# A mixer layer on one core: the last o block copied out between shifted blocks, the tail of g_b as one list, v and z in single transfers

## The chip, the cores and the metric

The kernel runs on one core of a Trainium2 chip, in one launch. The metric is the device time of one execution in microseconds. A core has five engines, each of which executes its own list of instructions in order and waits at semaphores for the others: TensorE (PE in the profile), VectorE (DVE), ScalarE (ACT), GpSimd (POOL) and SyncE (SP), whose list here consists of DMA issues.

## The reference, cut to what matters

512 prompt rows and 32 sample rows of width 2048 go through one layer. All weights are float32.

```python
h = rmsnorm(x, norm_w) * (1 + scl) + shift
q, k, v, o, z_a, ifg, u, z_b, g_a, g_b = split_cols(h @ w_in)
hm, c1, n1, m1 = mlstm_sequence(heads(q), heads(k) * DH ** -0.5, heads(v), ig, lf, c0, n0, m0)   # 4 heads of 512
a  = silu(z_a) * head_layernorm(sigmoid(o) * hm, head_norm_w)
pb, new_hist = pool_mixer(u, hist, pos0, w_pool_mix, pool_scale)   # 4 groups of 256 columns, windows 2, 4, 8, 16
bb = silu(z_b) * pb
merged = sigmoid(g_a) * (a @ w_branch_a) + sigmoid(g_b) * (bb @ w_branch_b)
y = rmsnorm(x + gate * (merged @ w_out), final_norm_w)
```

In `pool_mixer` a group takes the mean over its window of the last inputs (15 rows of history stand ahead of the first), subtracts the input and multiplies by a 256 x 256 matrix.

## The kernel before

Everything is kept with features on partitions and the T = 544 rows (512 + 32) along the free axis, in two halves of 272. A float32 product is made of three matmuls: `split` (L90 to L92) casts a tile to a high part on ACT and subtracts it on DVE for the low part, and PE adds up high x high, low x high and high x low in PSUM. This is done for weights (`whi`, `wlo`) and for activations (`h_hi`, `h_lo`) alike. A column block is 128 outputs wide; one with 16 k-tiles takes 16 x 3 x 2 = 96 matmuls. PSUM has a pool "mm" of two slots with two banks each, for the sums of a block, and a pool "ax" of four single banks, which `aux` hands out.

The stages follow one another in program order:

- Head 0 of k, q, v and o through `project` (L108 to L131), on h without its shift; their shift is added later as a bias. Each block's sums are copied to `ot` by ACT (L411) and stored to `d_p` from POOL's queue (L412).
- The shift of h: 16 k-tiles `hx` on DVE, split in place into `h_hi` and `h_lo` (L468 to L473), with PE taking up each tile at once for the input and forget gates (L477) and for the first two blocks of g_a (L484); the second half of block 1 follows at L491. Their weights come from `parts` (`whi` and `wlo`, 128 x 1024), with rows loaded by `load_rows`.
- Three more pairs of g_a blocks by `plain_pair` (L518), then the rest of the projection by `fast_pair` (L639, L651), which needs fewer products.
- The tail: the last four blocks of g_b, 12 to 15, again by `plain_pair` (L840 to L848). After a block its `evac` makes the sigmoid and calls `pool_group` (L782 to L839) for groups 0 and 1 behind block 13, for group 2 behind block 14 and for group 3 behind block 15. `pool_group` transposes the history and the last inputs on PE (`tp`, L797, L804, L805), sums the window on DVE (`lv`, one addition per doubling), subtracts (`dd`), splits (`d_hi`, `d_lo`), multiplies on PE into `mixed` (L834) and writes `zb` times `mixed` (L837) and its split `b_hi`, `b_lo`.
- The heads stage: blocks of branch_b (L1048), the filler, stand between the parts of each of the four heads: scores, `values` (transposes of v to rows, L948 and L952, out of tiles `vt`), `mix` (L961, L962), output gates from `o4`, norm, and `finish_head`, which multiplies by `zg`.
- The tiles `af` of the first three heads are read back and split (L1151), then branch_a and w_out.

The Tile framework puts the instructions of each engine in a list and the waits between them. A tile of a pool waits until the last user of its buffer is done. A DMA issue of SP that has to wait for its buffer holds every issue behind it in that list.

## Time and profile before

| what | value |
|---|---|
| median of 3 runs | 2283.69 us (2277.29, 2287.27, 2283.69) |
| the profiled execution | 2276.01 us |
| its span | 2274.2 us |
| mean granted clock of TensorE | 0.989 |
| busy share PE, DVE, ACT, POOL | 97 %, 72 %, 39 %, 5 % |
| mean DMA rate | 163 GB/s |

The span runs from the first to the last instruction of the profiled execution; its own time is 1.8 us more. A busy share is an average over all stages. The clock column of a window is TensorE's granted clock as a share of 2.4 GHz, the upper of its two levels; half of it is 1.2 GHz.

### The profile page before, as it was taken

The numbers are of one execution on the slowest core, as the hardware profiler recorded it, in microseconds if no ns is written. First come the engines' busy times: TensorE is split into PE (matmuls) and PEld (weight loads), VectorE is DVE, ScalarE is ACT, GpSimd is POOL, SyncE is SP. The second block draws the span as 40 slices with busy tenths as digits, with TensorE's granted clock in tenths as the row PEclk, the third lists the DMA queues.
The fourth block names the chain that finished last, engine by engine and source line by source line (L and its number), as shares of the span: only waits on it lengthen the run. The fifth ranks groups of instructions, "written<-read, shape, count | busy, mean of one in ns | idle before, by whom it ended". The sixth has DMA issues, their size and how long they took to land.

```text
span 2274.2 us, 40888 instructions
## 1 busy us (share of the span) xinstructions
PE 2200.9 (97%) x16767; PEld 2125.5 (93%) x16767; DVE 1645.2 (72%) x2432; ACT 897.7 (39%) x1486; POOL 117.3 (5%) x219
## 2 busy tenths in 40 slices
PE   6999989999999999999999999989999999999997
PEld 5789989999999999999999999978888899999997
DVE  6778698987798779877997777665556668774345
ACT  5532244443343343344443444434534432223334
POOL 0000010000000000000000000010011110000000
PEclk9999999999999999999999999989999999999999
DMA  6677643543454435533444334356655558675225
GB/s 221 217 223 245 194 133 97 173 146 121 137 159 151 141 113 165 165 119 125 143 160 138 115 121 142 113 163 211 214 193 195 177 171 264 212 220 181 84 85 162
DMA packets 321564, 370.04 MB, mean 163 GB/s; under 512 B 15777, under 2 KB 264957, under 8 KB 320161
## 3 DMA queue, kind: packets, MB, share of 16 engines
q1 hardware_dynamic: 299368, 310.77, 44.4%
q0 software_dynamic: 19856, 56.58, 6.8%
q8 instruction: 131, 2.15, 0.4%
q14 instruction: 57, 0.46, 0.1%
q10 hardware_dynamic: 2152, 0.08, 0.1%
HBM read 308.67 MB, written 58.67 MB: 162 GB/s over the span
## 4 chain that ended last, share of the span: by engine, by line
PE 80%; issue 11%; DMA 4%; DVE 2%; ACT 2%; POOL 1%; SPq 0%; DVEq 0%; ACTq 0%; POOLq 0%
PE mm L651 27%; PE mm L128 16%; PE d L651 11%; PE mm L130 8%; PE mm L530 5%; PE ca L961 2%; PE cb L962 2%; PE accp L371 2%; PE ada L279 1%; PE sc L906 1%; DMA side<-in_w_ada 1%; DMA vt<-d_p 1%; PE mm L484 1%; DMA af<-d_a 0%; PE accs L373 0%
## 5 line engine op out<-in xcount | busy, mean ns | idle before, releaser
L91 ACT CAST whi<-raw 128x512 fp32r<-128x512 f32 (+1 forms) x458 | 356.0, 784 | 684.6 <-PE mm L128 326.2
L92 DVE TENSOR_TENSOR wlo<-raw,whi 128x512 fp32r<-128x512 f32 (+1 forms) x458 | 404.9, 890 | 197.7 <-ACT whi L91 170.6
L651 PE MATMUL mm<-h_hi,whi 128*128 128x272 f32 x1600 | 466.1, 291 | 0.0
L651 PE MATMUL mm<-h_hi,wlo 128*128 128x272 f32 x1600 | 462.8, 289 | 0.0
L651 PE MATMUL mm<-h_lo,whi 128*128 128x272 f32 x1600 | 461.1, 288 | 0.0
L91 ACT CAST whi<-t 128x1024 fp32r<-128x1024 f32 x200 | 210.2, 1052 | 356.6 <-PE mm L651 324.7
L651 PEld LDWEIGHTS mm<-h_hi,whi 128*128 128x128 f32 x1600 | 301.0, 188 | 4.4 <-ACT y L691 0.3
L651 PEld LDWEIGHTS mm<-h_lo,whi 128*128 128x128 f32 x1600 | 301.6, 189 | 0.0
L651 PEld LDWEIGHTS mm<-h_hi,wlo 128*128 128x128 f32 x1600 | 301.4, 188 | 0.0
L92 DVE TENSOR_TENSOR wlo<-t,whi 128x1024 fp32r<-128x1024 f32 x200 | 244.6, 1224 | 76.0 <-ACT whi L91 74.3
L651 PE MATMUL d<-S_hi,wlo 128*128 128x272 f32 x800 | 233.1, 291 | 0.0
L651 PE MATMUL d<-S_hi,whi 128*128 128x272 f32 x800 | 230.2, 288 | 0.2 <-ACT whi L91 0.2
L651 PE MATMUL d<-S_lo,whi 128*128 128x272 f32 x800 | 229.7, 287 | 0.0
L651 PEld LDWEIGHTS d<-S_hi,wlo 128*128 128x128 f32 x800 | 150.2, 188 | 1.2
L651 PEld LDWEIGHTS d<-S_hi,whi 128*128 128x128 f32 x800 | 150.4, 188 | 0.6 <-ACT whi L91 0.6
L651 PEld LDWEIGHTS d<-S_lo,whi 128*128 128x128 f32 x800 | 150.4, 188 | 0.0
L636 DVE TENSOR_TENSOR t<-raw,t 128x1024 f32<-128x1024 f32 x100 | 122.2, 1222 | 2.2
L651 PE MATMUL mm<-S_hi,whi 128*128 128x272 f32 x400 | 120.6, 301 | 2.4 <-ACT whi L91 2.1
L658 DVE TENSOR_TENSOR u<-mm,m 128x272 f32<-128x272 f32 x100 | 44.1, 441 | 108.8 <-PE mm L651 108.5
L651 PE MATMUL mm<-S_hi,wlo 128*128 128x272 f32 x400 | 115.9, 290 | 0.0
L128 PE MATMUL mm<-m_hi,whi 128*128 128x272 f32 (+2 forms) x512 | 115.4, 291 | 0.1
L651 PE MATMUL mm<-S_lo,whi 128*128 128x272 f32 x400 | 115.4, 289 | 0.0
(417 smaller groups left out, 4728.2 us busy)
## 6 DMA issues: line engine op xcount, KB each, us to landing
raw<-in_w_in SPq DMA_DIRECT2D x112, 1024.0 KB, 5.4
side<-in_w_ada SPq DMA_DIRECT2D x64, 512.0 KB, 4.7
raw<-in_w_out SPq DMA_DIRECT2D x38, 512.0 KB, 3.9
raw<-in_w_ada SPq DMA_DIRECT2D x32, 512.0 KB, 4.6
braw<-in_w_in SPq DMA_DIRECT2D x64, 256.0 KB, 2.9
raw<-in_w_branch_a SPq DMA_DIRECT2D x32, 512.0 KB, 5.0
...
```

The costliest lines, as they stand in the source:

```text
L91: hi_ops.append(act.copy(out=hi, in_=src))
L92: return dve.tensor_tensor(out=lo, in0=src, in1=hi.bitcast(F32), op=ALU.subtract)
L128: pe.matmul(o, lhsT=whi[:, kk, :], rhs=mov[:, k, a:b], start=(k == 0 and mov is hi), stop=False)
L130: pe.matmul(o, lhsT=wlo[:, kk, :], rhs=hi[:, k, a:b], start=False, stop=(k == kt - 1))
L279: pe.matmul(ada[:, 0:2 * P], lhsT=cst[:, 4 * k:4 * k + P], rhs=w[:, kk, :], start=(k == 0 and w is parts[0]), stop=(k == KT - 1 and w is p ...
L371: pe.matmul(accp[d], lhsT=w[:, d * P:(d + 1) * P], rhs=x[:, j, 0:TP], start=first, stop=last)
L530: pe.matmul(acc[:, s, 0:HALF], lhsT=w[:, kk, :], rhs=mov[:, k, s * HALF:(s + 1) * HALF], start=(n == 0 and kk == 0 and x == 0), stop=(n == ...
L636: dve.tensor_tensor(out=t, in0=p, in1=q, op=op)
L651: pe.matmul(o, lhsT=w[i][:, k, :], rhs=x[j](k), start=start and k == 0 and n == 0, stop=k == HK - 1 and n == 2, skip_group_check=not start)
L658: dve.tensor_tensor(out=o, in0=p, in1=q, op=ALU.add)
L961: pe.matmul(ca[0:m, 0:HC], lhsT=l, rhs=r[:, 0:HC], start=first, stop=last)
L962: pe.matmul(cb[0:m, 0:VW - HC], lhsT=l, rhs=r[:, HC:VW], start=first, stop=last)
```

## The change

- **The last o block.** Its copy to `ot` and the store move from the projection loop into the shift loop, ahead of k-tile 4. Block 0 of g_a adds up in two aux banks and no longer in a slot of "mm", so that the sums of the last o block may stay in one slot while the gates take the other.
- **The tail.** `plain_pair` loses its order argument; the four blocks are written out as a list of eight half blocks, whose splits are issued two half blocks ahead. Group 0 comes behind block 13, groups 1 and 2 behind block 14, group 3 behind block 15. `mixed` takes two aux banks; its multiply is cut in two; the history of all groups is one tile `hists`; a block's sigmoid is one instruction of 544.
- **The heads.** The four v tiles of a head come in one transfer `v4`, issued with the next head's keys ahead of `mix`; the four z tiles come in one, `z4`, in the buffer of `o4`, behind the output gates.
- **af** has a pool of its own with three buffers.

```diff
--- before.py
+++ after.py
@@ -407,6 +407,8 @@
     for n, off in ((NQ, OFF_Q), (NV, OFF_V), (NO, OFF_O)):
         for d in range(DB):
             acc = project(w_in_, off + d * P, KT, h_hi, h_lo, side, 3)
+            if n == NO and d == DB - 1:
+                break
             ot = out_t.tile([P, T], F32, tag="ot", name="ot")
             act.copy(out=halves(ot), in_=acc)
             pool_e.dma_start(out=d_p[n, d], in_=ot)
@@ -463,9 +465,12 @@
     raw = [load_rows(w_in_, OFF_GA, half) for half in range(2)]
     wp = {(x // 2, x % 2): parts(raw[x // 2][:, :, x % 2 * P:(x % 2 + 1) * P]) for x in range(3)}
     accg = psum["mm"].tile([P, 2, 512], F32, tag="mm", name="mm")
-    acc0 = psum["mm"].tile([P, 2, 512], F32, tag="mm", name="mm")
-    accs = [[acc0[:, s, 0:HALF] for s in range(2)], [aux("d")[:, 0:HALF] for _ in range(2)]]
+    accs = [[aux("d")[:, 0:HALF] for _ in range(2)] for _ in range(2)]
     for j in range(KT):
+        if j == 4:
+            ot = yp.tile([P, T], F32, tag="sg", name="ot")
+            act.copy(out=halves(ot), in_=acc)
+            pool_e.dma_start(out=d_p[NO, DB - 1], in_=ot)
         hx = t2.tile([P, T], F32, tag="hx", name="hx")
         for g, (a, b) in enumerate(((0, TP), (TP, T))):
             dve.scalar_tensor_tensor(out=hx[:, a:b], in0=h_hi[:, j, a:b].bitcast(F32), scalar=mod[:, j, g:g + 1],
@@ -515,12 +520,12 @@
             split(sx, S_hi[:, :, j, :], S_lo[:, :, j, :])
             yield
 
-    def plain_pair(src, c0, evac, side, order=(0, 1)):
-
-        raw = {half: load_rows(src, c0, half) for half in order}
+    def plain_pair(src, c0, evac, side):
+
+        raw = [load_rows(src, c0, half) for half in range(2)]
         for blk in range(2):
             acc = psum["mm"].tile([P, 2, 512], F32, tag="mm", name="mm")
-            for n, half in enumerate(order):
+            for half in range(2):
                 whi, wlo = parts(raw[half][:, :, blk * P:(blk + 1) * P])
                 next(side, None)
                 for kk in range(HK):
@@ -528,7 +533,7 @@
                     for x, (w, mov) in enumerate(((whi, h_hi), (whi, h_lo), (wlo, h_hi))):
                         for s in range(2):
                             pe.matmul(acc[:, s, 0:HALF], lhsT=w[:, kk, :], rhs=mov[:, k, s * HALF:(s + 1) * HALF],
-                                      start=(n == 0 and kk == 0 and x == 0), stop=(n == 1 and kk == HK - 1 and x == 2))
+                                      start=(k == 0 and x == 0), stop=(k == KT - 1 and x == 2))
             evac(blk, [acc[:, s, 0:HALF] for s in range(2)])
 
     side = sums_of_halves()
@@ -779,14 +784,16 @@
     UL = HIST + TP + HIST + TS
     SH = HIST + TP
 
+    hists = pw.tile([HIST, D_B], F32, name="hists")
+    sp.dma_start(out=hists, in_=state_pool[0, 0])
+
     def pool_group(g):
         w = WINDOWS[g]
         wmix = pw.tile([P, 512], F32, tag="wmix", name="wmix").rearrange("p (b c) -> p b c", b=2)
         sp.dma_start(out=wmix, in_=w_pool_mix[0, g].rearrange("(b p) c -> p b c", p=P))
         wmh, wml = (pw.tile([P, 2, 256], F32R, tag=x, name=x) for x in ("wmh", "wml"))
         split(wmix, wmh, wml)
-        hist = pw.tile([HIST, 256], F32, tag="hist", name="hist")
-        sp.dma_start(out=hist, in_=state_pool[0, 0, :, g * 256:(g + 1) * 256])
+        hist = hists[:, g * 256:(g + 1) * 256]
         u = pw.tile([P, 2, UL], F32, tag="u", name="u", bufs=2)
         dve.memset(u[:, :, 0:HIST], 0.0)
         tp = aux("tp")
@@ -825,27 +832,47 @@
         split(dd, d_hi, d_lo)
         for c in range(2):
             ct = 2 * g + c
-            mixed = psum["mm"].tile([P, 2, 512], F32, tag="mm", name="mixed")
+            mixed = [aux("mixed")[:, 0:HALF] for _ in range(2)]
             for b in range(2):
                 lw = [(wmh[:, b, c * P:(c + 1) * P], (d_hi, d_lo)), (wml[:, b, c * P:(c + 1) * P], (d_hi,))]
                 for wn, (wt, movs) in enumerate(lw):
                     for mov in movs:
                         for s in range(2):
-                            pe.matmul(mixed[:, s, 0:HALF], lhsT=wt, rhs=mov[:, b, s * HALF:(s + 1) * HALF],
+                            pe.matmul(mixed[s], lhsT=wt, rhs=mov[:, b, s * HALF:(s + 1) * HALF],
                                       start=(b == 0 and wn == 0 and mov is d_hi), stop=(b == 1 and wn == 1))
             x = zb[:, c, :]
-            dve.scalar_tensor_tensor(out=halves(x), in0=mixed[:, :, 0:HALF], scalar=pscT[:, ct:ct + 1], in1=halves(x),
-                                     op0=ALU.mult, op1=ALU.mult)
+            for s in range(2):
+                dve.scalar_tensor_tensor(out=halves(x)[:, s, :], in0=mixed[s], scalar=pscT[:, ct:ct + 1],
+                                         in1=halves(x)[:, s, :], op0=ALU.mult, op1=ALU.mult)
             split(x, b_hi[:, ct, :], b_lo[:, ct, :])
-    for jj in range(KT // 2 - NTAIL, KT // 2):
-        def evac(blk, acc):
-            sg = yp.tile([P, T], F32, tag="sg", name="sg")
-            for s in range(2):
-                act.activation(out=sg[:, s * HALF:(s + 1) * HALF], in_=acc[s], func=AF.Sigmoid)
-            pool_e.dma_start(out=d_gb[2 * jj + blk], in_=sg)
-            for g in (((), (0, 1)), ((2,), (3,)))[jj - KT // 2 + NTAIL][blk]:
-                pool_group(g)
-        plain_pair(w_in_, OFF_GB + jj * 2 * P, evac, iter(()), (1, 0))
+    seq = [(ct, half) for ct in range(KT - 2 * NTAIL, KT) for half in (1, 0)]
+    raws = {}
+
+    def tail_parts(n):
+        ct, half = seq[n]
+        if ct % 2 == 0:
+            raws[half] = load_rows(w_in_, OFF_GB + ct * P, half)
+        return parts(raws[half][:, :, ct % 2 * P:(ct % 2 + 1) * P])
+
+    ready = [tail_parts(0), tail_parts(1)]
+    for n in range(0, len(seq), 2):
+        ct = seq[n][0]
+        acc = psum["mm"].tile([P, 2, 512], F32, tag="mm", name="mm")
+        for x, half in enumerate((1, 0)):
+            whi, wlo = ready.pop(0)
+            for kk in range(HK):
+                k = half * HK + kk
+                for y, (w, mov) in enumerate(((whi, h_hi), (whi, h_lo), (wlo, h_hi))):
+                    for s in range(2):
+                        pe.matmul(acc[:, s, 0:HALF], lhsT=w[:, kk, :], rhs=mov[:, k, s * HALF:(s + 1) * HALF],
+                                  start=(x == 0 and kk == 0 and y == 0), stop=(x == 1 and kk == HK - 1 and y == 2))
+            if n + 2 + x < len(seq):
+                ready.append(tail_parts(n + 2 + x))
+        sg = yp.tile([P, T], F32, tag="sg", name="sg")
+        act.activation(out=halves(sg), in_=acc[:, :, 0:HALF], func=AF.Sigmoid)
+        pool_e.dma_start(out=d_gb[ct], in_=sg)
+        for g in ((), (0,), (1, 2), (3,))[n // 2]:
+            pool_group(g)
     wctx.close()
     pctx.close()
     hctx.close()
@@ -1061,6 +1088,9 @@
         sp.dma_start(out=t, in_=d_p[n, h * DB:(h + 1) * DB].rearrange("d p t -> p d t"))
         return t
 
+    def load_values(h):
+        return load_four(h, NV, el.tile([P, DB, T], F32, tag="v4", name="v4"))
+
     def load_keys(h):
         return load_four(h, NK, fmajor(bigt("qk"))), load_four(h, NQ, fmajor(bigt("qk")))
 
@@ -1080,11 +1110,10 @@
             act.activation(out=kT, in_=kT, func=AF.Copy, scale=KSCALE)
         return scores(h, kT, qT)
 
-    def values(h):
+    def values(h, v4):
         v = v_tiles()
         for d in range(DB):
-            vt = el.tile([P, T], F32, tag="vo", name="vt", bufs=2)
-            sp.dma_start(out=vt, in_=d_p[NV, h * DB + d])
+            vt = v4[:, d, :]
             if h == 0:
                 add_bias(vt, NV, d)
             v_tokens(vt, *v, d)
@@ -1102,10 +1131,9 @@
         return so, sos
 
     def load_z(h):
-        zgs = [el.tile([P, T], F32, tag=f"zg{d}", name="zg") for d in range(DB)]
-        for d in range(DB):
-            sp.dma_start(out=zgs[d], in_=d_z[h * DB + d])
-        return zgs
+        z4 = el.tile([P, DB, T], F32, tag="o4", name="z4")
+        sp.dma_start(out=z4, in_=d_z[h * DB:(h + 1) * DB].rearrange("d p t -> p d t"))
+        return [z4[:, d, :] for d in range(DB)]
 
     def finish_head(h, hm, zgs):
         for d in range(DB):
@@ -1123,14 +1151,14 @@
     sco = start_head(0, *keys)
     c0 = load_state(0)
     fill(1)
-    v = values(0)
+    v = values(0, load_values(0))
     for h in range(H):
         o4 = load_four(h, NO, el.tile([P, DB, T], F32, tag="o4", name="o4"))
         if h + 1 < H:
-            keys = load_keys(h + 1)
+            keys, v4 = load_keys(h + 1), load_values(h + 1)
         hm = mix(h, c0, *sco, *v)
+        so, sos = out_gates(h, o4)
         zgs = load_z(h)
-        so, sos = out_gates(h, o4)
         fill(1)
         if h + 1 < H:
             head_norm(hm, so, sos)
@@ -1138,7 +1166,7 @@
             c0 = load_state(h + 1)
             fill(1)
             finish_head(h, hm, zgs)
-            v = values(h + 1)
+            v = values(h + 1, v4)
             fill(1)
     mctx.close()
     bigctx.close()
@@ -1146,8 +1174,10 @@
     a_hi = hpool.tile([P, KT, T], F32R, tag="h_hi", name="a_hi")
     a_lo = hpool.tile([P, KT, T], F32R, tag="h_lo", name="a_lo")
     head_norm(hm, so, sos)
+    actx = ctx.enter_context(ExitStack())
+    afp = actx.enter_context(tc.tile_pool(name="afp", bufs=3, side="right", reuse_waits="tile"))
     for k in range(KT - DB):
-        af = el.tile([P, T], F32, tag="vo", name="af", bufs=2)
+        af = afp.tile([P, T], F32, tag="af", name="af")
         sp.dma_start(out=af, in_=d_a[k])
         split(af, a_hi[:, k, :], a_lo[:, k, :])
         if k % 4 == 3:
@@ -1160,6 +1190,7 @@
     dve.tensor_copy(out=nst, in_=tp[0:H * DB, 0:2 * P].rearrange("p (g c) -> p g c", g=2))
     for g, dst in enumerate((n_prompt, n_sample)):
         pool_e.dma_start(out=dst[0, 0].rearrange("h (r p) -> (h r) p", p=P), in_=nst[:, g, :])
+    actx.close()
     rctx.close()
 
 
```

What the lists of the engines make of it is shown at four places. ACT around the last o block, before (`ot` is the copy of a block's sums, `hx` a shifted k-tile, `raw` and a number the weights of g_a):

```order
L91 CAST whi<-raw 128x512
L411 COPY ot<-mm 128x544
L91 CAST whi<-raw 128x512
L411 COPY ot<-mm 128x544
L91 CAST whi<-raw_3046 128x1024 x2
L91 CAST whi<-raw_3048 128x1024
L91 CAST h_hi<-hx 128x544 x13
L91 CAST whi<-raw_3048 128x1024
```

And with the change:

```order
L413 COPY ot<-mm 128x544
L91 CAST whi<-raw 128x512
L91 CAST h_hi<-hx 128x544 x6
L91 CAST whi<-raw_3043 128x1024 x2
L91 CAST whi<-raw_3045 128x1024
L472 COPY ot<-mm 128x544
L91 CAST h_hi<-hx 128x544 x8
L91 CAST whi<-raw_3045 128x1024
```

The copy of the last block stood ahead of the weight casts and of all `h_hi` casts; it now stands behind six `h_hi` casts and three weight casts.

PE between blocks 13 and 14 of g_b, before (`tp` are the transposes of a pooling group, `mixed` its product):

```order
L805 MATMUL tp<-ident,u 15x128
L797 MATMUL tp<-ident,hist 128x15 x2
L804 MATMUL tp<-ident,u 15x128
L805 MATMUL tp<-ident,u 15x128
L804 MATMUL tp<-ident,u 15x128
L805 MATMUL tp<-ident,u 15x128
L797 MATMUL tp<-ident,hist 128x15 x2
L834 MATMUL mixed<-d_hi,wmh 128x272 x4
L804 MATMUL tp<-ident,u 15x128
L834 MATMUL mixed<-d_lo,wmh 128x272 x2
L834 MATMUL mixed<-d_hi,wml 128x272 x2
```

With the change, the first matmuls of the same stage, L867 being those of the blocks:

```order
L867 MATMUL mm<-h_lo,whi 128x272 x2
L867 MATMUL mm<-h_hi,wlo 128x272 x2
L804 MATMUL tp<-ident,hists 128x15 x2
L811 MATMUL tp<-ident,u 15x128
L812 MATMUL tp<-ident,u 15x128
L811 MATMUL tp<-ident,u 15x128
L812 MATMUL tp<-ident,u 15x128
L867 MATMUL mm<-h_hi,whi 128x272 x2
L867 MATMUL mm<-h_lo,whi 128x272 x2
```

And a little on, where the first group's product begins:

```order
L867 MATMUL mm<-h_hi,wlo 128x272 x2
L867 MATMUL mm<-h_hi,whi 128x272 x2
L841 MATMUL mixed<-d_hi,wmh 128x272 x4
L867 MATMUL mm<-h_lo,whi 128x272 x2
L867 MATMUL mm<-h_hi,wlo 128x272 x2
L867 MATMUL mm<-h_hi,whi 128x272 x2
L841 MATMUL mixed<-d_lo,wmh 128x272 x2
L841 MATMUL mixed<-d_hi,wml 128x272 x2
```

Two groups were executed without a block's matmul between them; now 22 rows of block 14 stand between the transposes of group 0 and its `mixed`, and more of them between the parts of `mixed`.

SP's queue in a head, before (`qk` are the next head's keys and queries, `raw` weights of branch_b, `gh` gate rows, `sgb` a stored g_b block):

```order
L1061 DMA qk<-d_p 128x4x544
L87 DMA raw<-in_w_branch_b 128x8x128
L1061 DMA qk<-d_p 128x4x544
L884 DMA gh<-rows_g 128x544
L1050 DMA sgb<-d_gb 128x544
L1087 DMA vt<-d_p 128x544 x2
L1107 DMA zg<-d_z 128x544 x4
L1087 DMA vt<-d_p 128x544 x2
L87 DMA raw<-in_w_branch_b 128x8x128
```

With the change:

```order
L1135 DMA z_17536<-d_z 128x4x544
L1088 DMA qk<-d_p 128x4x544 x2
L911 DMA gh<-rows_g 128x544
L1077 DMA sgb<-d_gb 128x544
L87 DMA raw<-in_w_branch_b 128x8x128 x2
L1088 DMA o_17974<-d_p 128x4x544
L1088 DMA v_17980<-d_p 128x4x544
L1077 DMA sgb<-d_gb 128x544
```

The `vt` and `zg` loads of one head, eight issues, have become one `z` load and one `v` load, the latter for the head after.

## Rows read from the trace of the kernel before

**Rows 1.** The page, part 1: busy time, share of the span, instructions of each engine.
```profile
PE 2200.9 (97%) x16767; PEld 2125.5 (93%) x16767; DVE 1645.2 (72%) x2432; ACT 897.7 (39%) x1486; POOL 117.3 (5%) x219
```

**Rows 2.** PE's waits over the span: engine, line, releaser, total us, times, longest.
```profile
PE tp L948 <- DMA vt<-d_p: 9.0, 4, 3.6
...
PE mm L477 <- ACT h_hi L91: 6.7, 1, 6.7
```

**Rows 3.** Windows near 290: us, PE, PEld, DVE, ACT, POOL, clock, DMA, GB/s.
```profile
270.00:280.00 10.00, 10.00 (x82) 10.00 (x82) 3.51 (x9) 2.05 (x5) 0.54 (x1) 1.00 0.92 283
...
280.00:290.00 10.00, 4.90 (x40) 4.68 (x38) 3.47 (x4) 3.44 (x4) 0.54 (x1) 0.93 0.25 90
...
290.00:300.00 10.00, 8.38 (x52) 8.35 (x53) 10.00 (x22) 4.22 (x7) 0.00 (x0) 0.73 0.34 104
```

**Rows 4.** Timeline of ACT, 276 to 300: start, us, instruction, idle before, releaser.
```profile
284.94 0.61 ACT L411 COPY ot<-mm 128x544 f32<-128x544 f32 x1 [8.65 <-PE mm L130]
...
285.45 2.94 ACT L91 CAST whi<-raw 128x1024 fp32r<-128x1024 f32 x3
```

**Rows 5.** Timeline of DVE, the same stretch.
```profile
286.53 3.50 DVE L92 TENSOR_TENSOR wlo<-raw,whi 128x1024 fp32r<-128x1024 f32 x3 [9.51 <-ACT whi L91]
...
291.60 0.72 DVE L92 TENSOR_TENSOR h_lo<-hx,h_hi 128x544 fp32r<-128x544 f32 x1
...
294.53 0.72 DVE L92 TENSOR_TENSOR h_lo<-hx,h_hi 128x544 fp32r<-128x544 f32 x1
```

**Rows 6.** Windows of the tail and of the heads stage.
```profile
1506.60:1529.80 23.20, 13.07 (x74) 10.72 (x73) 20.58 (x31) 9.23 (x18) 5.00 (x9) 0.78 0.40 114
...
1530.00:1540.00 10.00, 10.00 (x69) 10.00 (x69) 8.32 (x9) 2.32 (x4) 0.00 (x0) 0.83 0.19 57
...
1600.00:1610.00 10.00, 8.94 (x59) 8.58 (x60) 5.84 (x14) 7.20 (x14) 0.00 (x0) 0.83 1.00 309
...
1668.00:1672.00 4.00, 3.80 (x21) 3.70 (x22) 1.33 (x4) 1.89 (x6) 0.00 (x0) 0.62 0.69 227
...
1736.00:1740.00 4.00, 4.00 (x35) 3.97 (x34) 2.67 (x6) 1.65 (x4) 0.54 (x1) 1.00 0.89 280
```

**Rows 7.** Timeline of PE in the tail and in head 0, three of its waits.
```profile
1513.97 1.27 PE L834 MATMUL mixed<-d_hi,wmh 128*128 128x272 f32 x4 [2.38 <-ACT d_hi L91]
...
1563.57 0.51 PE L128 MATMUL mm<-b_hi,whi 128*128 128x272 f32 x2 [1.89 <-ACT whi L91]
...
1600.70 0.66 PE L948 MATMUL tp<-ident,vt 128*128 128x128 f32 x4 [3.01 <-DVE vt L1072]
```

**Rows 8.** DVE by line, 1500 to 1535: busy us, mean ns, idle before.
```profile
L815 DVE TENSOR_TENSOR lv<-lv 128x1142 f32<-128x1142 f32 (+1 forms) x4 | 5.4, 1346 | 0.1
...
L822 DVE SCALAR_TENSOR_TENSOR dd<-lv,u 128x64 f32<-128x64 f32 (+1 forms) x6 | 4.1, 719 | 0.0
...
L92 DVE TENSOR_TENSOR d_lo<-dd,d_hi 128x1088 fp32r<-128x1088 f32 x3 | 3.9, 1284 | 0.0
...
L837 DVE SCALAR_TENSOR_TENSOR zb<-mixed,pscT,zb 128x544 f32<-128x544 f32 x4 | 3.0, 779 | 1.4 <-PE mixed L834 1.4
```

**Rows 9.** ACT by line, the same stretch.
```profile
L91 ACT CAST d_hi<-dd 128x1088 fp32r<-128x1088 f32 x3 | 3.3, 1097 | 2.9 <-DVE dd L822 2.9
```

**Rows 10.** Tile vt: DVE's bias operations, ns min/median/max.
```profile
L1072 DVE TENSOR_SCALAR vt<-vt,bias x8: 230/356/487, 1580.7 to 1602.1; 128x512 f32<-128x512 f32 x4, 128x32 f32<-128x32 f32 x4
```

**Rows 11.** Timeline of SP's queue in the tail and in head 1.
```profile
1532.87 18.04 SPq L800 DMA_DIRECT2D zb<-d_zb  x2
...
1558.70 0.37 SPq L87 DMA_DIRECT2D raw<-in_w_branch_b  x1
...
1669.53 1.84 SPq L1087 DMA_DIRECT2D vt<-d_p  x2
```

**Rows 12.** Timeline of PE in the heads stage, two of its waits.
```profile
1734.25 0.63 PE L948 MATMUL tp<-ident,vt 128*128 128x128 f32 x4 [3.63 <-DMA vt<-d_p]
...
1841.00 0.52 PE L130 MATMUL mm<-b_hi,wlo 128*128 128x272 f32 x2 [1.56 <-DVE wlo L92]
```

## The prediction

> **What bounds the kernel now.** I read the page first: TensorE (PE) is busy for 97 % of the span [rows 1], so the end is set by the length of PE's own list, and a change that adds or removes hardly any matmul can gain only where PE stands idle or runs at a low granted clock. Next comes the list of PE's waits [rows 2]: 9.0 us for `vt` from DMA in four waits of the heads stage, 6.7 us in one wait for `h_hi` at L477. Then the windows say what such a place costs in all, the clock with it: at full speed 82 matmuls start in 10 us, 0.122 us each; in 280 to 300 it is 40 and 52 [rows 3]. The timelines of ACT and DVE tell who was late, and the windows of the later stages what else is lost.
>
> **Place 1, the last o block.** ACT executes in order. Its copy of `ot` at L411 waits 8.65 us for PE to end the block, the three casts `whi` (2.94 us, 0.98 each) follow it, and only then do the casts `h_hi` begin [rows 4]. DVE in the same way idles 9.51 us, does three `wlo` (3.50 us, 1.17 each), then shifts two tiles of h in the 2.93 us from 291.60 to 294.53, 1.46 each [rows 5]. PE loses (82 - 40) + (82 - 52) = 72 starts, 8.8 us. In the ACT rows of the change six `h_hi` casts stand ahead of the three `whi`, and the copy stands behind them; so six tiles (8.8 us of DVE) are shifted while PE is still in the block. What stays: the `whi` casts still find their buffer read by PE until the block ends, so the first weight pair needs 0.98 + 1.17 = 2.15 us, against ten matmuls of the gate columns (L477) that can go first, 1.2 us: 0.9 lost, and as much again if the sixth tile comes late. The gain is 8.8 - 1.8 = **7.0**. If only four tiles are ready, the `whi` casts stand behind two more (2.9 us): 4.1 at the least; 8.8 at most. Moving the copy costs nothing: its two accumulator banks are not needed until the next plain pair, since block 0 now accumulates in two aux banks; its cast and store (0.61 us of ACT, one issue on POOL's queue) run beside matmuls, and one more k-tile of h waits 0.6 us behind it with six in hand.
>
> **Place 2, the tail of g_b and the pooling.** From 1506.6 to 1529.8 PE executes 74 instructions [rows 6], which at 0.122 are 9.0 us: 14.2 lost, because both pooling groups stand between blocks 13 and 14 and PE waits for each link, 2.38 us for `d_hi` for example [rows 7]. The clock is 0.83 in the 10 us behind it: 69 starts, 13 short, 1.6 us [rows 6]. Then 1.89 us for the first `whi` of branch_b [rows 7]: 17.7 in all. The change puts 44 to 46 matmuls of a block between the transposes of a group and its `mixed` for groups 0, 1 and 2, and some 68 of branch_b for group 3. New waits, from the DVE and ACT rows [rows 8, 9]: group 2 has three `lv` (4.05), two `dd` (1.44), `d_hi` (1.10), and half of the group before's two `zb` (0.78 each) and two `b_lo` (as `h_lo`, 0.72 each, the same 128x544 [rows 5]), 1.5: 8.1 against 45 x 0.122 = 5.5, so 2.6. Group 3 has four `lv`: 9.4 against 8.3, so 1.1. `d_lo` follows `d_hi` by 1.28 with 8 matmuls to cover it in group 2 (0.3 left) and 4 in group 3 (0.8 left, and five bias operations of 0.36 ahead of it on DVE [rows 10], 1.8). The weights of branch_b are still issued when block 15 lets its raw buffers go: 4.87 us from issue to first matmul (1558.70 to 1563.57) [rows 7, 11], less 2.6 + 0.5 that PE spends on group 2: 1.8. New waits 8.4; the place gains 17.7 - 8.4 = **9.3**. The bounds: 3.8 if the 5.5 that cover one group are lost too; 17.7 with no new wait. One `hists` transfer for four, one sigmoid for two and splits two ahead: nothing on the path in groups 0 and 1, where the block covers them. Splitting the `zb` multiply adds an instruction on DVE per column block; DVE has over 1.5 us of slack per group there.
>
> **Place 3, the v tiles.** In head 0 PE waits 3.01 us for DVE's `vt` [rows 7], and 1600 to 1610 has 59 starts in 8.94 busy us where 73 fit, 1.7 more [rows 6]. The bias work on v stays on DVE; I keep 2.3 of new wait (between 0 and the 3.01 of the row, nearer to it): **2.4** gained. In heads 1 to 3 the 9.0 of [rows 2] ends, and the slow stretch 1668 to 1672 with 21 starts in 3.80 us where 31 fit, 1.2 [rows 6]: `v4` is asked for a whole head before its use instead of behind four `zg` loads on SP's queue. What is late next is the chain that empties a tile's aux banks, `vh` on ACT and `vl` on DVE, some 1.2 us a head (as `d_hi` plus nothing else of [rows 9]; bounds 0 and 3.0): 10.2 - 3.6 = **6.6**, from 1.2 to 10.2. The load of `z4` now waits in SP's queue for the transposes of the output gates; behind it stand the next keys and `gh`, which no instruction of PE needs before the head in hand is done. **Place 4**, three `af` buffers: of the 1.56 us at 1841.00 [rows 12] 1.0 (0 to 1.6).
>
> Sum: 7.0 + 9.3 + 2.4 + 6.6 + 1.0 = **26.3**. Against the profiled execution, 2276.0, that is 2249.7. The median of the runs shown is 7.7 above that execution, the lowest 1.3; I add 2.3: **2252**.
>
> **Clock.** Behind one wait for `vt`, in 1668 to 1672, the clock is 0.62; behind the wait of 3.63 us that ends at 1734.25 it is 1.00 [rows 6, 12]. Waits of one kind thus cost 1.2 us more or nothing. The Trainium skill (TensorE: Matmul & The Clock Gate, Part 1: The HAM clock gate) says that the throttled clock is the default, that activity releases it, and that the place of the gate's window differs from run to run; the trace agrees, with its 0.62 and 1.00. By that rule the new waits of place 2 would be paid twice in some executions, as in the first rival.
>
> **Rivals.** (a) The pooling stays a chain. `mixed` now takes two of the four aux banks, and each is held until DVE's multiply has read it: if the transposes of the next group wait for that, 2 x 0.78 for each of four groups, 6.2, and twice a clock loss as at 1668 (1.2): 8.6 less gain, **2260.6**. For it: DVE is busy 20.58 of 23.20 us there [rows 6]; against it: the blocks between give DVE 5.5 us a group. (b) The v wait changes its name: the transfers are early, but transposes wait for the banks' copies as long as now. The heads gain 1.0: **2257.6**. For it: the 3.01 of head 0 was DVE, not DMA; against it: the longest waits end with a DMA. (c) Place 1 does not do what it says: the tiles hx reuse memory that the store of the eleventh block still reads, so the shift starts late and the `whi` casts queue behind it; gain 1.0, **2258.0**. (d) Slower: SP's queue stands. `z4` waits in it for `o4`, and weights, keys and `gh` queue behind. It decides from the point where PE waits 10.8 us in each of four heads, 43 us in all: **2295**. For it: the vt waits come from this very order, the second pair of `vt` issued at 1669.53 behind four `zg` [rows 11]; against it: SP stood 18.04 us at `zb` [rows 11] and PE lost 1.89 by it. The Trainium skill (DMA: Bandwidth & Descriptors, Anatomy of one DMA) says that a semaphore wait is spent on the issuing sequencer, ahead of dispatch, so that everything behind it is held. That speaks for (d); the 18.04 agree.
>
> **How the numbers follow.** A measurement of this kernel can tell about 0.5 %, 11.4 us, from no change: faster means under 2272.3, slower over 2295.1. The forecast has 0.62, (a) 0.12, (b) 0.09, (c) 0.05, all of them faster, any two together too (2266 for a and b): 0.88. All three together, for they share ACT's and DVE's turns, give 2272 and more: 0.09 for no difference. (d) has 0.03. The range: the gains at their best together (8.8 + 17.7 + 4.7 + 10.2 + 1.6) are 43, which would need every new wait to vanish; I go two thirds of the way from 26.3, to 37.5, and leave out the 2.3: 2238. On the other side it ends beyond two rivals together, at 2270.
>
> **What would show it.** Place 1: no PE wait over 1 us near 285, the `ot` copy behind six `h_hi` casts, the last plain g_a blocks 7 us earlier. Place 2: no window under 60 starts between blocks 13 and 15; PE waits for `d_hi`, `d_lo` and `whi` of some 8 us between block 14's end and group 3. Place 3: no PE wait for DMA of v; waits of about 1 us for aux banks. Wrong would be waits of over 15 us in place 2, a DMA wait in the heads stage, or windows at a clock under 0.8 in it.

## The result

The changed kernel took 2245.14 us (median of 4 runs, 2241.78 to 2250.89) against 2282.82 for the kernel before (4 runs): a ratio of 0.985, 95 % interval 0.9832 to 0.9869, or some 34 us less. The profiled execution took 2246.56 us, its span is 2244.8; that is 29.4 less than the span before. The forecast was 2252 with a range of 2238 to 2270.

PE's share of the span is 98 % [rows 1], with the same 16767 instructions:

```profile
PE 2195.6 (98%) x16767; PEld 2121.1 (94%) x16767; DVE 1646.7 (73%) x2440; ACT 893.6 (40%) x1478; POOL 117.8 (5%) x219
```

The list of PE's waits over the span (engine, line, releaser, total us, times, longest), without those at the start of the program:

```profile
PE mixed L841 <- ACT d_hi L91: 4.5, 2, 3.0
...
PE d L489 <- ACT whi L91: 2.1, 1, 2.1
```

The 9.0 us for `vt` and the 6.7 us for `h_hi` [rows 2] are gone. So is a wait in the tail that the same list of the kernel before has, of a block's first matmul for DVE's multiply of `mixed`:

```profile
PE mm L530 <- DVE zb L837: 3.4, 1, 3.4
```

The 4.5 us for `d_hi` in the tail were 2.6 in the kernel before. New are the 2.1 us for `whi` at L489, where the shifted blocks begin. The waits for `wlo` at L130, in the branches, are 4.6 us where 3.9 stood.

To see where the time came from I cut the span at four instructions of PE that both kernels have. The view of a line gives the first and the last start of its instructions. These are the plain g_a pairs, the fast pairs, the numerators `ca` and the transposes of `finish`, first in the kernel before (there L530 has the tail's blocks too, so only its first start counts), then in the changed kernel:

```profile
L530 PE MATMUL mm<-h_hi,whi x320: 285/288/429, 325.6 to 1557.9; 128*128 128x272 f32 x160
...
L651 PE MATMUL mm<-h_hi,wlo x1600: 282/289/297, 399.5 to 1481.0; 128*128 128x272 f32 x178
...
L961 PE MATMUL ca<-vh,se x80: 276/282/416, 1604.5 to 1819.4; 128*128 128x256 f32 x80
...
L1039 PE MATMUL tp<-ident,hm x64: 270/272/330, 1654.8 to 1859.9; 128*128 128x128 f32 x64
```

```profile
L535 PE MATMUL mm<-h_hi,whi x192: 286/288/290, 319.5 to 391.0; 128*128 128x272 f32 x192
...
L656 PE MATMUL mm<-h_hi,wlo x1600: 282/289/296, 393.3 to 1475.3; 128*128 128x272 f32 x178
...
L988 PE MATMUL ca<-vh,se x80: 277/282/388, 1587.5 to 1789.6; 128*128 128x256 f32 x80
...
L1066 PE MATMUL tp<-ident,hm x64: 270/273/329, 1636.5 to 1832.8; 128*128 128x128 f32 x64
```

| stretch | before | changed | gain | forecast |
|---|---|---|---|---|
| A: end of the last o block to the first plain g_a matmul | 40.7 | 36.0 | 4.7 | 7.0 |
| plain and fast pairs | 1155.4 | 1155.8 | -0.4 | 0 |
| T: end of the fast pairs to the first `ca` of head 0 | 123.5 | 112.2 | 11.3 | 9.3 + 2.4 |
| H: first `ca` to the last transpose of `finish` | 255.4 | 245.3 | 10.1 | } 6.6 + 1.0 |
| E: from there to the end | 414.3 | 412.0 | 2.3 | } |

The o block's end is the first start of the gate matmuls, 283.5 in the changed kernel; in the kernel before that start, 291.6, stands behind the wait of 6.7, so 284.9. What is left of the 29.4, some 1.4, was there before the o block ended: PE's waits for the first loads (`xt` and others) differ from run to run. The cuts do not hold the same work in both kernels, since the order of PE's list changes: T has 741 PE instructions before and 756 changed, H 1757 and 1747, E 3183 and 3178. At 0.122 us each [rows 3], an estimate for the same work is 13.1 us of gain in T, 8.9 in H and 1.7 in E.

**A in the changed kernel.** Windows (columns as in [rows 3]), first the two near 290, then the tail:

```profile
280.00:290.00 10.00, 7.92 (x55) 7.70 (x54) 10.00 (x18) 6.03 (x9) 0.34 (x1) 0.88 0.05 15
...
290.00:300.00 10.00, 10.00 (x78) 10.00 (x78) 10.00 (x21) 4.28 (x7) 1.94 (x3) 0.95 1.30 306
...
1510.00:1520.00 10.00, 10.00 (x82) 9.79 (x81) 6.15 (x9) 3.24 (x7) 1.01 (x2) 1.00 0.25 88
...
1520.00:1530.00 10.00, 10.00 (x79) 9.60 (x79) 6.97 (x14) 3.12 (x6) 0.67 (x3) 1.00 0.30 89
...
1530.00:1540.00 10.00, 6.55 (x44) 6.01 (x43) 8.27 (x12) 3.29 (x5) 1.68 (x3) 0.84 0.71 207
...
1540.00:1550.00 10.00, 9.68 (x63) 9.25 (x63) 7.11 (x12) 6.57 (x14) 1.10 (x2) 0.82 0.82 272
...
1550.00:1560.00 10.00, 7.31 (x54) 6.66 (x53) 9.26 (x19) 2.09 (x4) 0.00 (x0) 1.00 1.02 304
```

280 to 290 has 55 starts where 40 stood, 290 to 300 has 78 where 52 stood [rows 3]. The copy of `ot` and the casts on ACT:

```profile
285.37 0.65 ACT L91 CAST h_hi<-hx 128x544 fp32r<-128x544 f32 x1 [0.18 <-DVE hx L476]
...
285.92 2.94 ACT L91 CAST whi<-raw 128x1024 fp32r<-128x1024 f32 x3
...
288.76 0.60 ACT L472 COPY ot<-mm 128x544 f32<-128x544 f32 x1
```

DVE in the same stretch, its first shift and the `h_lo` of the fourth and of the sixth tile:

```profile
277.67 1.74 DVE L476 SCALAR_TENSOR_TENSOR hx<-h_hi,mod,h_lo 128x512 f32<-128x512 f32 x4 [1.88 <-DMA d_p<-ot]
...
283.57 0.72 DVE L92 TENSOR_TENSOR h_lo<-hx,h_hi 128x544 fp32r<-128x544 f32 x1
...
286.53 0.72 DVE L92 TENSOR_TENSOR h_lo<-hx,h_hi 128x544 fp32r<-128x544 f32 x1
```

And PE:

```profile
284.52 0.41 PE L482 MATMUL mm<-h_hi,wst 128*128 128x272 f32 x2
...
287.01 0.52 PE L489 MATMUL d<-h_hi,whi 128*128 128x272 f32 x2 [2.08 <-ACT whi L91]
...
289.29 0.66 PE L489 MATMUL d<-h_hi,wlo 128*128 128x272 f32 x2
```

DVE's shift starts at 277.67, after a wait of 1.88 us for the store of an earlier o block. The fourth tile is done at 284.3 and the sixth at 287.2, while PE leaves the o block at 283.5: some four tiles, and not six, are shifted under the block. PE finishes the gate matmuls of the tiles it has at 284.9 and then waits 2.08 us for `whi`: ACT casts the fifth and the sixth tile first, until 286.0, and takes the weight cast only then, though PE had left the o block, and with it their buffer, 2.4 us earlier. The last row takes 0.66 us in place of the 0.41 of the first: the wait cost clock as well.

**T.** The windows from 1510 to 1530 have 82 and 79 starts; in the kernel before 1506.6 to 1529.8 had 74 in all [rows 6]. The loss sits behind block 15 now, 44, 63 and 54 starts. PE's timeline there:

```profile
1537.67 1.27 PE L841 MATMUL mixed<-d_hi,wmh 128*128 128x272 f32 x4 [2.99 <-ACT d_hi L91]
...
1539.41 0.82 PE L128 MATMUL mm<-b_hi,whi 128*128 128x272 f32 x2 [0.46 <-ACT whi L91]
...
1556.64 0.77 PE L841 MATMUL mixed<-d_hi,wmh 128*128 128x272 f32 x4 [1.51 <-ACT d_hi L91]
...
1558.19 0.52 PE L841 MATMUL mixed<-d_lo,wmh 128*128 128x272 f32 x2 [0.78 <-DVE d_lo L92]
```

**H.** No PE wait over 0.25 us stands between 1590 and 1810. The v loads, and the idle time before instructions on v that ended with `vl`, 1.1 us in five waits:

```profile
L1088 SPq DMA_DIRECT2D v<-d_p x4: 370/420/499, 1563.1 to 1709.8; - x4
...
  DVE vl L92: 1.1, 5
```

The four loads of v go out between 1563.1 and 1709.8; the last transpose of v starts at 1768.4. SP's queue in head 0, where the next keys stand behind the `z` load, and the next load of v:

```profile
1619.49 17.45 SPq L1088 DMA_DIRECT2D qk<-d_p  x2
...
1650.92 0.50 SPq L1088 DMA_DIRECT2D v<-d_p  x1
```

SP stood 17.45 us at the keys, and PE waited for nothing behind it.

### The profile page after: what moved, and what is told of

Same layout as the page of the kernel before. It is cut to its first block, busy times and chain, and to the rows that moved or that the text cites. A ratio compares the mean times of both kernels' runs of the same rounds, so it can differ in the third digit from the quotient of the medians.

```text
span 2244.8 us, 40831 instructions
## 1 busy us (share of the span) xinstructions
PE 2195.6 (98%) x16767; PEld 2121.1 (94%) x16767; DVE 1646.7 (73%) x2440; ACT 893.6 (40%) x1478; POOL 117.8 (5%) x219
## 4 chain that ended last, share of the span: by engine, by line
PE 79%; issue 13%; DMA 3%; DVE 3%; ACT 2%; POOL 1%; SPq 0%; ACTq 0%; DVEq 0%; POOLq 0%
PE mm L656 27%; PE mm L128 15%; PE d L656 11%; PE mm L130 7%; PE mm L535 3%; PE ca L988 2%; PE cb L989 2%; PE accp L371 2%; PE mm L867 2%; PE ada L279 1%; PE sc L933 1%; PE d L489 1%; DVE wlo L92 1%; DMA side<-in_w_ada 1%; PE accs L373 0%
## 5 line engine op out<-in xcount | busy, mean ns | idle before, releaser
L663 DVE TENSOR_TENSOR u<-mm,m 128x272 f32<-128x272 f32 x100 | 44.1, 441 | 109.5 <-PE mm L656 109.1
```

Of the source, the lines that this page charges most:

```text
L663: dve.tensor_tensor(out=o, in0=p, in1=q, op=ALU.add)
```

## The experiments

Each kernel was timed in rounds with the kernel before; the ratio is to that kernel. Since a few us of 2250 are hardly more than the ratios' intervals, the stretches of the table above are taken from each run's profile as well. Kernels with the same code in a stretch differ by up to 1.7 us in A, 5.2 in T, 2.9 in H and 3.5 in E (1.4 without u_tail), so a difference of one kernel counts where it is larger than that or where a wait in its rows explains it. The two longest T of the same code, u_af and a_order4, have a granted clock of 0.94 over T, the others 0.97. T also holds 755 to 762 PE instructions where the tail is the changed one, but 739 in u_tail and 732 in t_mm, which have the rest in H: 2 to 3 us.

| kernel | ratio, 95 % interval | A | T | H | E |
|---|---|---|---|---|---|
| before | 1 | 40.7 | 123.5 | 255.4 | 414.3 |
| changed | 0.985 (0.9832 to 0.9869) | 36.0 | 112.2 | 245.3 | 412.0 |
| u_oblock | 0.9879 (0.9865 to 0.9893) | 41.1 | 111.5 | 245.3 | 412.3 |
| u_tail | 0.9926 (0.991 to 0.9942) | 35.9 | 118.3 | 248.2 | 415.0 |
| u_heads | 0.9922 (0.9909 to 0.9935) | 34.5 | 112.9 | 258.5 | 412.9 |
| u_af | 0.9869 (0.9853 to 0.9886) | 34.6 | 116.7 | 243.9 | 414.5 |
| t_mm | 0.9935 (0.9921 to 0.9949) | 34.4 | 125.7 | 247.5 | 411.7 |
| t_g01 | 0.9858 (0.9843 to 0.9873) | 35.8 | 109.5 | 247.3 | 412.5 |
| t_mixonly | 0.9946 (0.9926 to 0.9966) | 40.6 | 110.9 | 259.5 | 414.1 |
| h_late | 0.9867 (0.985 to 0.9884) | 34.4 | 112.7 | 244.3 | 412.3 |
| h_vtwo | 0.9899 (0.9876 to 0.9921) | 36.1 | 112.7 | 251.6 | 412.7 |
| a_order4 | 0.9856 (0.9834 to 0.9877) | 33.5 | 115.7 | 246.5 | 412.9 |
| b_g01 | 0.9839 (0.9817 to 0.9861) | 33.5 | 110.7 | 247.0 | 411.5 |
| b_early | 0.9848 (0.9827 to 0.987) | 33.8 | 114.7 | 246.1 | 411.9 |

### Each part undone alone

The part's diff is taken back in the changed kernel, the rest stays. **u_oblock:**

```diff
-            if n == NO and d == DB - 1:
-                break
...
-    accs = [[aux("d")[:, 0:HALF] for _ in range(2)] for _ in range(2)]
+    acc0 = psum["mm"].tile([P, 2, 512], F32, tag="mm", name="mm")
+    accs = [[acc0[:, s, 0:HALF] for s in range(2)], [aux("d")[:, 0:HALF] for _ in range(2)]]
...
-        if j == 4:
-            ot = yp.tile([P, T], F32, tag="sg", name="ot")
```

> The changed kernel with its first part undone: the last o block is copied in the projection loop again and block 0 of g_a adds up in a slot of mm. If the parts add up, as my sum takes it, this gives back what the marker rows of the two traces show for that place: the first matmul of the plain g_a pairs stands 6.1 us earlier in the changed kernel, 1.25 of which were there before the o block ended, so about +5 us against the changed kernel (near 2250 where that is 2245), a PE wait of 6 to 7 us for h_hi, and no difference in any later stage. The rival, that the time won there is given back later (the later stages wait for the same loads), gives +1 us or less.

A is 41.1 again, the other stretches are the changed kernel's, and PE's wait is back:

```profile
PE mm L477 <- ACT h_hi L91: 6.7, 1, 6.7
```

The part gives 5 us (by the medians' ratios 0.0029, 6.6 us, with intervals that overlap by 0.0004), and nothing of it is taken back later.

**u_tail:** `plain_pair` with its order, `pool_group` with `hist` and `mixed` as before.

```diff
-    hists = pw.tile([HIST, D_B], F32, name="hists")
...
-            mixed = [aux("mixed")[:, 0:HALF] for _ in range(2)]
+            mixed = psum["mm"].tile([P, 2, 512], F32, tag="mm", name="mixed")
...
-    seq = [(ct, half) for ct in range(KT - 2 * NTAIL, KT) for half in (1, 0)]
+    for jj in range(KT // 2 - NTAIL, KT // 2):
```

> The changed kernel with its second part undone: plain pairs, two pooling groups behind block 13, mixed in mm. If the parts add up it is about 9 us slower than the changed kernel (forecast for the tail alone 9.3, near 2254), with the PE waits for hist, d_hi and zb of before back and a window near 1510 with 25 to 40 starts in 10 us. The rival, that the new waits of the tail (3.0, 1.5 and 0.8 us in the changed kernel's trace, and the slow clock behind them) eat most of the gain, gives 3 us or less.

The waits for `zb` and for the history are back, as in the kernel before:

```profile
PE mm L535 <- DVE zb L842: 3.4, 1, 3.4
...
PE tp L802 <- DMA hist<-in_state_pool: 2.9, 2, 1.9
```

T is 6.1 longer, and some 8 for the same work, since 17 PE instructions fewer stand in it. H and E together are 5.9 longer, in code that is the changed kernel's; some 2 of it are those instructions, and no row explains the rest. The time is 0.0076 of 2283 or 17 us longer, more than the 9 expected. The rival, under 3 us, falls.

**u_heads:** `values` with `vt` in two buffers, `load_z` with four `zg`, ahead of the output gates.

```diff
-            vt = v4[:, d, :]
+            vt = el.tile([P, T], F32, tag="vo", name="vt", bufs=2)
+            sp.dma_start(out=vt, in_=d_p[NV, h * DB + d])
...
-        so, sos = out_gates(h, o4)
         zgs = load_z(h)
+        so, sos = out_gates(h, o4)
```

> The changed kernel with its third part undone: v in four loads at their use, z in four. If the DMA waits for v were the loss, it is about 10 us slower than the changed kernel (lead in the heads stage 10.1 us by the traces, 9.0 us of waits before and 1.2 of slow clock), near 2255, with PE waits for vt from DMA of 7 to 9 us. The rival of my forecast, that transposes of v would wait for their banks in any case, gives 1 to 6.6 us.

H is 13.2 longer and the waits are back:

```profile
PE tp L975 <- DMA vt<-d_p: 9.2, 3, 3.7
...
PE tp L975 <- DVE vt L1099: 0.6, 1, 0.6
```

The rival of the forecast falls: in the changed kernel, where the data are there early, the transposes of v do not wait for their banks. Head 0 is another matter. Its wait for DVE's `vt`, 3.01 us in the kernel before [rows 7], is 0.6 here with v as before, and T is only 0.7 longer than in the changed kernel: with the new tail the old transfers of v cost head 0 hardly anything.

**u_af:**

```diff
-        af = afp.tile([P, T], F32, tag="af", name="af")
+        af = el.tile([P, T], F32, tag="vo", name="af", bufs=2)
```

> The changed kernel with its fourth part undone: af in two buffers of the pool el. The forecast gave this part 1.0 us (0 to 1.6); the traces show 2.3 us of lead from the end of the heads stage to the end of the run. If that is the third buffer, this kernel is 1 to 2.3 us slower; if the lead comes from waits elsewhere (a wait for wlo of 1.4 us at 1889 in the kernel before), it is within 0.5 us of the changed kernel.

In the whole time inconclusive. E is 2.5 longer, but H 1.4 shorter, and `af` is read in both: H + E is 658.4 against 657.3, where kernels with the third buffer and the same heads have 656.6 to 659.8 (u_tail 663.2). The ratios' intervals overlap. The rows say more of the wait from which the forecast took its 1.0, 1.56 us for `wlo` in the kernel before [rows 12]. Here it is first in this kernel, then in the changed one:

```profile
1811.79 0.52 PE L130 MATMUL mm<-b_hi,wlo 128*128 128x272 f32 x2 [1.57 <-DVE wlo L92]
```

```profile
1812.43 0.52 PE L130 MATMUL mm<-b_hi,wlo 128*128 128x272 f32 x2 [2.73 <-DVE wlo L92]
```

All eleven kernels with the third buffer have 2.20 to 2.85 us there, the three with two buffers 1.56 or 1.57. The third buffer makes this wait longer. What it brings elsewhere is not shown.

### Which edit of the tail

**t_mm**, one edit taken back in the changed kernel:

```diff
-            mixed = [aux("mixed")[:, 0:HALF] for _ in range(2)]
+            mx = psum["mm"].tile([P, 2, 512], F32, tag="mm", name="mixed")
+            mixed = [mx[:, s, 0:HALF] for s in range(2)]
```

> The changed kernel with one edit of the tail undone: mixed is one tile of the pool mm again, in place of two aux banks. All other edits of the tail stay (list of half blocks, splits ahead, groups behind blocks 13, 14, 14 and 15, one hists). Theory: which PSUM pool mixed comes from decides, since a mixed tile in mm takes the slot that the next block needs, and the order of PE's list then puts whole groups between blocks as before; it gives back nearly all of the tail's gain, 7 to 11 us slower than the changed kernel, like the kernel with the whole part undone. Rival: the places of the groups and the earlier splits bring the gain; then 0 to 3 us slower.

PE's waits in the tail, and the window 1505 to 1530, first of this kernel, then of the changed one:

```profile
1509.32 1.27 PE L842 MATMUL mixed<-d_hi,wmh 128*128 128x272 f32 x4 [5.44 <-ACT d_hi L91]
...
1541.74 0.82 PE L868 MATMUL mm<-h_hi,whi 128*128 128x272 f32 x2 [3.61 <-DVE zb L846]
```

```profile
1505.00:1530.00 25.00, 20.07 (x146) 19.49 (x147) 23.64 (x34) 6.71 (x11) 3.32 (x6) 0.86 0.33 91
```

```profile
1505.00:1530.00 25.00, 25.00 (x198) 24.34 (x197) 16.26 (x29) 8.37 (x14) 2.04 (x5) 1.00 0.32 98
```

In 1505 to 1530 it has 146 starts where the changed kernel has 198. The whole gain of T is given back (125.7), with every other edit of the tail still in, and the time is 0.0085 or 19 us longer, more than the 7 to 11 expected. T is 7.4 longer than in u_tail (118.3), which has `mixed` in mm too: beside a `mixed` in mm the other edits of the tail lengthen this stretch, though the whole times of the two kernels do not differ clearly. So the 13.5 is what this edit is worth among the others, and the parts do not add up. The wait for `zb` shows how: the block behind the groups needs the slot of "mm" that `mixed` holds until DVE's multiply has read it, so PE's list has whole groups with no block's matmul among them.

**t_g01:**

```diff
-        for g in ((), (0,), (1, 2), (3,))[n // 2]:
+        for g in ((), (0, 1), (2,), (3,))[n // 2]:
```

> The changed kernel with another edit of the tail undone: groups 0 and 1 both behind block 13, group 2 behind 14 and group 3 behind 15; mixed stays in aux. Theory as for the kernel with mixed in mm: the pool decides, so this stays within 2 us of the changed kernel. Rival, the places of the groups decide: 7 to 11 us slower. In the order of PE's list the groups are one to a block here as well.

T is 109.5 and the ratio is within the changed kernel's interval: which of these two places the groups are called from does not matter. In PE's list the groups stand one to a block here as well. The waits behind block 15 changed their names, from `d_hi` to the weights of branch_b:

```profile
1537.01 0.52 PE L128 MATMUL mm<-b_hi,whi 128*128 128x272 f32 x2 [1.23 <-ACT whi L91]
...
1540.89 0.57 PE L130 MATMUL mm<-b_hi,wlo 128*128 128x272 f32 x2 [3.12 <-DVE wlo L92]
```

**t_mixonly**, the kernel before with the one edit:

```diff
-            mixed = psum["mm"].tile([P, 2, 512], F32, tag="mm", name="mixed")
+            mixed = [aux("mixed")[:, 0:HALF] for _ in range(2)]
...
-            dve.scalar_tensor_tensor(out=halves(x), in0=mixed[:, :, 0:HALF], scalar=pscT[:, ct:ct + 1], in1=halves(x),
+            for s in range(2):
+                dve.scalar_tensor_tensor(out=halves(x)[:, s, :], in0=mixed[s], scalar=pscT[:, ct:ct + 1],
```

> The kernel before with one edit alone: mixed in two aux banks with its multiply in two halves. The order of PE's list then has the groups between the parts of a block, as in the changed kernel. Theory, the pool decides: from the end of the fast pairs to the first ca the kernel before took 123.5 us, the changed kernel 112.2, the one with mixed back in mm 125.7; this one takes 110 to 115 and is 8 to 13 us faster than the kernel before, with the vt waits of the heads as they were. Rival, splits ahead and one history transfer are needed as well: 118 or more, under 5 us faster.

The same window (this kernel ends its fast pairs at 1482.9, 7.6 us later):

```profile
1505.00:1530.00 25.00, 25.00 (x198) 24.39 (x197) 16.54 (x25) 8.47 (x15) 3.41 (x6) 1.00 0.30 88
```

T is 110.9, 12.6 less than before, and the time 0.0054 or 12 us less. The waits for `vt` are 7.6 us where 9.0 stood. In the profiled execution H is 4.1 longer than before, at a clock of 0.97 in place of 0.99, so its span is only 6.8 less. Taken back alone it costs the tail's gain, done alone it brings it: this edit is shown to be the cause. What splits ahead, one history and one sigmoid add was not seen in any stretch: T is 112.2 with them.

### Which edit of the heads

**h_late:**

```diff
-            keys, v4 = load_keys(h + 1), load_values(h + 1)
+            keys = load_keys(h + 1)
...
-            v = values(h + 1, v4)
+            v = values(h + 1, load_values(h + 1))
```

> The changed kernel with v still one transfer a head, but asked for when the values are made, and not a head ahead. If the asking ahead is what ends the waits, PE waits for v in heads 1 to 3 and this gives back most of the 10 us of the heads stage, 5 to 10 us slower than the changed kernel. If the single transfer and the loads of z that no longer stand ahead of it are what matters, 0 to 2 us slower.

H is 244.3, there is no wait for v, and the ratio's interval overlaps the changed kernel's. The line that asks ahead does nothing: SP's list has the v load at the same place in both kernels, right behind the load of o. Here it goes out 0.42 us after that load, as the one at 1650.92 does in the changed kernel:

```profile
1647.80 0.57 SPq L1088 DMA_DIRECT2D v<-d_p  x1
```

The tile has a buffer of its own, which lets the framework issue its load when that is free.

**h_vtwo**, v as before, z as in the change:

```diff
-            vt = v4[:, d, :]
+            vt = el.tile([P, T], F32, tag="vo", name="vt", bufs=2)
+            sp.dma_start(out=vt, in_=d_p[NV, h * DB + d])
```

> The changed kernel with v as before (four transfers a head into two buffers, asked for when used) and z as in the change (one transfer behind the output gates). The kernel that asked for v4 late lost nothing, and SP's list in it has the v load of a head at the same place as the changed kernel, since a buffer of its own lets it go early. Theory, buffers: with two buffers the second pair of v waits for the first to be used, so PE waits for vt from DMA come back, 4 to 9 us in heads 1 to 3, and the heads stage (first ca of head 0 to the last transpose of finish, 245.3 in the changed kernel, 258.5 with the whole part undone) is 251 to 258. Rival, the four z loads that stood ahead of the second pair were the cause: no wait for vt over 1 us, and 244 to 247.

```profile
PE tp L975 <- DMA vt<-d_p: 6.3, 4, 2.4
```

H is 251.6, between the two. Theory and rival share it: 6.3 us (251.6 - 245.3) go with v in four transfers and two buffers, as much as its waits. That the buffers do it, and not the four transfers, was not tried apart; in SP's list the second pair of a head goes out 6.0 us behind the first (1642.37 and 1648.38). The other 6.9 (258.5 - 251.6) go with the z loads, as one transfer and behind the output gates, which was not taken apart further; the ratios alone do not tell this kernel from u_heads.

### Place 1 and versions of the change

**a_order4:**

```diff
+    last_cast = hi_ops[-1].ins
...
-        split(hx, h_hi[:, j, :], h_lo[:, j, :])
+        with tc.issue_after(last_cast) if j >= 4 else ExitStack():
+            split(hx, h_hi[:, j, :], h_lo[:, j, :])
```

> The changed kernel with the h_hi casts of k-tiles 4 and on queued on ACT behind the three weight casts, so that four and not six h_hi casts stand ahead of the weights. In the changed kernel PE waits 2.08 us for whi at 287.01, and 287 to 291 goes at the lower clock. Theory: the casts ahead on ACT (the sixth ends at 286.0, the weight cast starts at 285.92) hold the first weights back, PE leaves the o block at 283.5 and the gates at 284.8; with four ahead the first whi is ready near 284.9, the wait falls to 0.5 us at most, and the first plain g_a matmul comes 2 to 3 us earlier: 2 to 3 us faster than the changed kernel. Rival: the weight casts wait for the buffer that the o block's last matmuls read until PE reports its end later than that; then the wait stays near 2 us and the time is the same.

ACT has the weight casts behind four tiles now, and they wait only for PE's end of the o block:

```profile
283.06 0.65 ACT L91 CAST h_hi<-hx 128x544 fp32r<-128x544 f32 x1 [0.23 <-DVE hx L477]
...
284.19 2.94 ACT L91 CAST whi<-raw 128x1024 fp32r<-128x1024 f32 x3 [0.48 <-PE mm L128]
```

PE's next wait is for `wlo`:

```profile
287.91 0.52 PE L491 MATMUL d<-h_hi,wlo 128*128 128x272 f32 x2 [1.15 <-DVE wlo L92]
```

The wait for `whi` is gone, and 1.15 us for `wlo` has come in its place, which was not expected. A is 33.5: 7.2 less than before. Against kernels with the change's own order it is 1.0 (34.4 to 34.6) or 2.5 (35.8 to 36.1) less: that order loses the clock in some executions and in others not, and this one, in three executions (33.5, 33.5, 33.8), did not. In the whole time it cannot be told.

**b_g01** and **b_early** have this order, and the groups as `((), (0, 1), (2,), (3,))` or `((0,), (1,), (2, 3), ())`.

> The changed kernel with groups 0 and 1 behind block 13 and with the h_hi casts from k-tile 4 on behind the weight casts on ACT. Both alone were within the measurement of the changed kernel; by the stages the first took 109.5 against 112.2 from the fast pairs' end to the first ca, the second 33.5 against 36.0 from the o block's end to the plain pairs. If both hold, it is 3 to 5 us faster than the changed kernel. Rival: those differences are the clock's, which falls or not by the same wait (four kernels with the same code there have 34.4 to 34.6, three 35.8 to 36.0), and the time is the same.

> As the kernel with both edits, but with group 0 behind block 12, group 1 behind 13 and groups 2 and 3 behind block 14, so that all pooling chains start under a block's matmuls. Expected: the d_hi waits behind block 15 (3.0 and 1.5 us in the changed kernel) and the slow clock of 1530 to 1550 (38 and 19 starts short of 82) go, and 107 to 110 us from the fast pairs' end to the first ca: 4 to 7 us faster than the changed kernel. Rival: the wait for branch_b's weights, which cannot be asked for before block 15 ends, takes their place (4.9 us from issue to first matmul, with some 3 us of mixed to cover it), and it is the same as the other.

b_g01 has the lowest median of all, 2243.03 us, and the ratio 0.9839, but its interval holds the changed kernel's 0.985: no difference that can be told. In b_early the rival came true, with T at 114.7 where 107 to 110 was expected. The waits for `d_hi` behind block 15 are gone, and one longer wait takes their place:

```profile
1543.50 0.82 PE L128 MATMUL mm<-b_hi,whi 128*128 128x272 f32 x2 [8.48 <-ACT whi L91]
```

ACT's cast of these weights, first in b_early, then in the changed kernel:

```profile
1542.83 0.62 ACT L91 CAST whi<-raw 128x512 fp32r<-128x512 f32 x1 [7.15 <-DMA raw<-in_w_branch_b]
```

```profile
1538.74 1.14 ACT L91 CAST whi<-raw 128x512 fp32r<-128x512 f32 x2 [1.12 <-DMA raw<-in_w_branch_b]
```

The first weights of branch_b are asked for at 1535.05 in b_early and at 1534.72 in the changed kernel, so from issue to cast it is 7.8 us in the one and 4.0 in the other, and 8.45 to the first matmul where the kernel before had 4.87 [rows 7, 11]. Why they took so long is open: two loads of keys, 1088 KB each, stand 0.42 us behind in both. ACT's list has this cast ahead of the last group's `d_hi`, which could not fill the gap either: its input was ready at 1539.5, and it was cast at 1543.35.

## Why the prediction was right

The range held the time, and the stretches bear most of the sum out, but not each step.

- **Place 1**, 7.0 forecast, 4.7 seen. As said, the copy behind the weight casts cost nothing. The step that failed is "six tiles (8.8 us of DVE) are shifted while PE is still in the block". By the forecast's own rows that did not fit: DVE's idle time began at 277.0 (286.53 - 9.51) and PE let the copy go at 284.94 [rows 4, 5], 7.9 us. The store of rival (c) took 1.88 more, and some four tiles were ready at the end. So the forecast's lower bound came, 4.1, with the weight casts behind two more `h_hi` casts: 2.08 us of wait, against its sign of none over 1 us, and some 1.5 of slow clock in this execution. a_order4 showed what the order costs: with four casts ahead of the weights the place gains 7.2.
- **Place 2 and head 0**, 11.7 forecast, 11.3 seen. The new waits were priced at 8.4; those in the trace between block 15 and group 3 are 2.99 + 0.46 + 0.32 + 0.40 + 1.51 + 0.78 = 6.5, and the clock of 0.84 and 0.82 in two windows takes more. 2.6 for group 2's `d_hi` was 2.99, 1.1 for group 3's was 1.51. The 2.3 kept for head 0's v was 0.2: too cautious; and u_heads shows that the new tail ends most of that wait without the new transfers of v. That the pooling lay in one chain was read rightly; the reason, the slot of "mm", I named only as a move of banks, and had rival (a) look for harm in it. t_mm and t_mixonly showed this one edit to bring the whole gain.
- **Place 3**, 6.6 forecast, and 1.0 for af: together 7.6, and 12.4 seen. The 1.2 of new wait a head did not come; H gains 10.1 where 10.2 was the most [rows 2, 6]. Of the reason I gave, "asked for a whole head before its use instead of behind four `zg` loads", the first half is not the reason: h_late asks late and loses nothing, since a buffer of its own lets the load go early. The z loads out of the way are about half of the 13.2 of u_heads.
- **Place 4**, 1.0 forecast. The step failed: the wait that it was to shorten went from 1.56 to 2.73. E gains 2.3 all the same, some 0.6 of it instructions that moved to other stretches; where the rest comes from is open.
- **The rivals.** (b) and (d) fell: no wait for banks; SP stood 17.45 us and no wait of PE followed. (a) fell: it is the other way about. (c) was true in its cause, a wait of 1.88 us of DVE, and in its effect in part: the `whi` casts did queue behind late tiles, and 4.7 of gain was left where it said 1.0.

That the sum came so near is in part luck, since misses cancelled: place 1 gave 2.3 less and place 3 with 4 some 4.8 more than forecast, and 1.4 of the 29.4 lie ahead of every place.
